# Moving the gate tiles and the gathers, powers and scatters within a loop over 32 experts

## The chip, the cores and the metric

The kernel runs on one core of a Trainium2 chip. The metric is the device time of one execution in microseconds. The kernel before takes 1062.58 us, the median of three runs (1060.21 to 1063.12).

## The reference, cut to what matters

One layer of a streaming encoder for 1024 tokens of width 1024. A mixer (three kinds of heads) adds to `h`; then a mixture of 32 experts adds to it, two experts per token; at the end a gate, computed from the sum, adds an embedding. Only the last two parts matter here.

```python
def hierarchical_moe(h, ...):
    ...
    y = routed_experts(xt, e_idx, e_w, w_gate, w_up, w_down)

def block_ffn(args):
    tok, wt, e = args
    xb = xt[tok]
    hb = jax.nn.silu(xb @ w_gate[e]) * (xb @ w_up[e])
    return (hb @ w_down[e]).astype(F32) * wt[:, None]

def reference(...):
    ...
    h = h + hierarchical_moe(rms_norm(h, norm2_g[i]), ...)
    gate = jax.nn.sigmoid(rms_norm(h, ple_norm_g[i]) @ ple_gate_w[i])
    h = h + gate * (p[i] @ ple_proj_w[i]).astype(F32)
    return rms_norm(h, final_g).astype(x.dtype)
```

A row of the output needs the sum of both its experts, so the gate can be computed for those tokens first whose second expert comes early.

## The kernel before, in words

Up to about 600 us the kernel computes the mixer and the routing. Then comes the stage that the change touches: a loop `for e in range(NE - 1)` over experts 0 to 30 (L1807), and behind it, from 992 us to the end, expert 31 and the last three gate tiles.

**An expert.** Each has at most 128 tokens. `gather` (L1226, GpSimd) fetches their rows from the DRAM tensor `hn2s` into one of three buffers `xg`, three experts ahead. `turned` (L1239) transposes them on TensorE; `up` (24 matmuls, L144 to L146) multiplies by the gate and up weights, `act` applies the activation, `hidden` transposes the result (`ph`, L1258), `down` (12 matmuls) multiplies by the down weight one loop later. `scaled` (L1275, ScalarE) writes the output times the routing weight into `yo`, of which there are two (`NYO`). `scatter` (L1278, GpSimd) adds these rows in DRAM to `h2s`, the sum for all tokens. Each scatter waits for the one before, since both add to the same tensor.

**Weights.** All matmuls take fp16 pairs. A weight arrives in fp32 by a transfer of 1 MB that SyncE issues, into one of the free buffers `ws` or `arena`; `split` then makes the pair: ScalarE the high half (L140), VectorE the low half (L141). A buffer is free again behind the split. `refill(e)`, at the top of the loop, issues as many transfers of the list `parts` as there are free buffers. That list holds the three weights of each expert, in order. `KEEP(e)` says how many buffers `refill` has taken out of this circulation by loop e: they later hold the gate's weight, the projection's weight and the gate tiles (`slot`, `new_set` at the loops in `SETS`).

**The gate.** The gate's weight (four quarters) and the projection of the embedding are split in the loops of `GW` (one loop later, by `GLAG`), a quarter a loop: five extra splits. Tokens are put into the order of their second expert: `ranks` (L1634, L1636, GpSimd) and `ranked` (L1641, TensorE) in loop 2, `reorder` in loops 3 to 6. The tokens form eight tiles of 128. Tile t has a pair (L, C) in `TILES`, and `add` puts its steps at named points of the loops:

- `load` at loop L: two GpSimd gathers by the tile's order (L1692), of the rows of `p` into `pin` and of the rows of `h2s` into `h3`. The second needs the scatters up to expert `AFTER[t]`, and no later one.
- `rms` at L + 2: ScalarE squares (L1709), VectorE scales (L129), GpSimd takes the power (`rg`, L131). `norm` at L + 2: VectorE multiplies (L1713). `embed` at L + 2: two transposes (`ptr`, L1718) and a small split.
- `turned` at C: eight transposes (`h3t`, L1725) and two splits. `mm` at C and C + 1: 24 matmuls each, half a tile. `emb`, `gate`, `square` and `gained` (L1762, GpSimd) beside them.
- `out` at C + 2: another power (`rf`). `send`: L1779 on VectorE and an indirect write to the output (L1783, GpSimd).

Tiles 0 to 4 have their steps in the loop, tiles 5 to 7 behind it.

**The order.** Inside `tc.manual_schedule` every engine runs its instructions in the order in which the program is written. A loop's points are, in order: `refill`, scatter, gather, `up`, point "up", `act`, the next expert's `turned`, point "turned", the last expert's `down`, the first weight split of expert e+2, point "mid", its second split, point "late", `hidden`, point "emb", the split of the down weight, a gate split, `scaled`, point "gate". The scatter in loop e is that of expert e-2, the gather that of expert e+3. GpSimd issues gathers, scatters, tile loads and output writes from one instruction stream, in which the powers and the ranks' adds also stand.

Of the kernel before, what the change touches and what calls it, by code (L numbers as in the profile page):

```python
# [52 lines left out]
MMP = ("mid", "mm")  # L53
AFTERW = 1
HS = 16.0
RMS = (2, "mid")
NORM = (2, "late")
EMB = (2, "mid")
TURN = (0, "up")
PPD = "emb"  # L60
# [1 line left out]
CUT = 320  # L62
NDW = 2
NYO = 2
GW = {6: (0,), 7: (1,), 8: (2,), 9: (3,), 10: (4,)}
GLAG = 1
TAIL = 4
RANK = 2
SETS = (9, 30)
TILES = ((10, 13), (14, 17), (17, 21), (21, 24), (25, 28))  # L70
AFTER = (8, 12, 14, 19, 23, 28, 30)
# [1 line left out]
_p = defaultdict(list)  # L73
def add(k, *ops): _p[k] += ops
for t, (L, C) in enumerate(TILES):
    add((L, "turned"), ("load", t))
    add((L + RMS[0], RMS[1]), ("rms", t))
    add((L + NORM[0], NORM[1]), ("norm", t))
    add((L + EMB[0], EMB[1]), ("embed", t))
    add((C + TURN[0], TURN[1]), ("turned", t))  # L80
    for i in range(2):
        add((C + i, MMP[i]), ("mm", t, i))
        add((C + i, PPD), ("emb", t, i))
        add((C + i, "gate"), ("gate", t, i), ("square", t, i), ("gained", t, 512 * i, 512 * i + 512))
    add((C + 2, OUT), ("out", t))
    add((C + 2, "gate"), ("send", t))
add((30, "turned"), ("load", 5))
PLAN = dict(_p)

KEEP = lambda e: min(8, max(0, e - 4))  # L90
HALVES = {3: (0,), 4: (1,), 5: (2,), 6: (3,), 7: (4, 5), 8: (6, 7)}
FOUR = {mybir.EngineType.PE, mybir.EngineType.Activation, mybir.EngineType.DVE, mybir.EngineType.Pool}

# [2 lines left out]
def hybrid_kernel(ctx, tc, x, p, norm1_g, w_in, conv_w, conv_b, igate_b, fgate_b, mnorm_g, sb_out_g,  # L96
# [27 lines left out]
    def rows(src, n):  # L124
        return bass.AP(tensor=src.tensor, offset=src.offset, ap=[[0, P], [1, n]])
# [1064 lines left out]
    class Expert:  # L1190
# [86 lines left out]
        def scatter(self):  # L1277
            return nc.gpsimd.indirect_dma_start(  # L1278
                out=h2s, out_offset=bass.IndirectOffsetOnAxis(ap=self.tb[:, 1:2], axis=0),
                in_=self.yo, in_offset=None, bounds_check=S - 1, oob_is_err=False, compute_op=OP.add)  # L1280
# [53 lines left out]
    for e in range(NE):  # L1334
        if e + 2 < NE:
            parts += [(e + 2, 0), (e + 2, 1)]
        if e:
            parts += [(e, 2)]
        parts += [(NE, a) for a in GW.get(e, ())]

# [234 lines left out]
    def at_e(e, f, *a):  # L1575
        if 0 <= e < NE:
            getattr(E[e], f)(*a)
# [3 lines left out]
    with tc.If(over > CAP):  # L1581
        with tc.tile_pool(name="ovc", bufs=1, side="right") as ovc:
            xo = ovc.tile([P, 2, KT, P], F16, name="xTo")
            late = ovc.tile([1, 1], F32, name="late")
# [31 lines left out]
    def refill(e):  # L1616
        while retired[0] < KEEP(e) and ready:
            retired[0] += 1
            kept.append(ready.pop(0))
        feed(min(len(ready), len(parts)))  # L1620
# [3 lines left out]
    def slot():  # L1624
        return (kept or ready).pop(0)


    def ranks():
        R.s = yaf[:, :2 * D]
        f = R.s.bitcast(F16).rearrange("p (a t e) -> p a t e", a=8, e=NE)  # L1630
        R.own, R.acc = f[:, 0, :NT], f[:, 1, :NT]
        nc.vector.tensor_copy(R.own[:, :, 0:1], LE[:, :, 0:1])
        nc.vector.tensor_tensor(R.own[:, :, 1:], LE[:, :, 1:], LE[:, :, :-1], op=OP.subtract)
        nc.gpsimd.memset(R.acc[:, 0], 0.0)  # L1634
        for t in range(1, NT):
            nc.gpsimd.tensor_tensor(R.acc[:, t], R.acc[:, t - 1], R.own[:, t - 1], op=OP.add)  # L1636
# [162 lines left out]
    def plan(e, point):  # L1799
        for f, t, *a in PLAN.pop((e, point), ()):  # L1800
            getattr(G[t], f)(*a)

    with tc.manual_schedule(engines=FOUR):
        nc.scalar.activation(jk[:, :1], vf32[:, n, 1, 2:3], AF.Silu)
        E[0].turned()
        E[0].split_d()
        for e in range(NE - 1):  # L1807
            refill(e)
            scatter(e - 2)
            at_e(e + NX, "gather")  # L1810
            if e == RANK:
                ranks()
            if RANK < e <= RANK + 4:
                reorder(2 * (e - RANK - 1), 2 * (e - RANK - 1) + 1)
            if e == RANK + 6:
                nc.gpsimd.dma_start(order, perm.rearrange("(t q) c -> q t c", q=P))
                nc.gpsimd.dma_start(fg, rows(final_g, D))
            E[e].up()
            plan(e, "up")
            E[e].act()  # L1820
            E[e + 1].turned()
            if e == NE - 2:
                E[e + 1].dw = [w.rearrange("p (k n) -> p k n", k=2) for w in slot().bitcast(F16).rearrange("p (a n) -> a p n", a=2)]
                E[e + 1].split_d()
            if e - 1 in SHIFT:
                E[e - 1].split_d()
            plan(e, "turned")
            plan(e, "mm")
            at_e(e - 1, "down")
            if e == RANK:  # L1830
                ranked()
            if e + 2 < NE:
                E[e + 2].split_g(0)
            plan(e, "mid")
            if e + 2 < NE:
                E[e + 2].split_g(1)
            plan(e, "late")
            E[e].hidden()
            plan(e, "emb")
            if e and e not in SHIFT:  # L1840
                E[e].split_d()
            for a in GW.get(e - GLAG, ()):
                gate_w(a) if a < 4 else proj_w()
            if e in SETS:
                new_set()
            at_e(e - 1, "scaled")
            plan(e, "gate")
            plan(e, "end")
        a, z = NE - 2, NE - 1
        scatter(a - 1)  # L1850
        E[z].up()
        E[z].act()
        G[5].embed("7")
        E[a].down()
        E[a].scaled()
        scatter(a)
        E[z].hidden()
        G[5].rms()
        G[5].norm()
        G[6].load(1)  # L1860
        E[z].down()
        E[z].scaled()
        scatter(z)
        G[5].turned("01")
        G[7].load(0, 0)
        G[5].mm(0, "23")
        G[5].emb(0, "7")
        G[5].gate(0)
        G[5].square(0)
        G[6].embed("0")  # L1870
        G[6].rms()
        G[6].norm()
        G[5].mm(1, "23")
        G[5].emb(1, "4")
        G[6].turned("01")
        G[5].gate(1)
        G[5].square(1)
        G[6].mm(0, "23")
        G[6].emb(0, "7")
        G[5].out()  # L1880
        G[5].send()
        G[6].gate(0)
        G[6].square(0)
        G[7].embed("0")
        G[7].rms()
        G[7].norm()
        G[6].mm(1, "23")
        G[6].emb(1, "4")
        G[7].turned("01")
        G[6].gate(1)  # L1890
        G[6].square(1)
        G[7].emb(0, "7")
        G[7].mm(0, "23")
        G[6].out()
        G[6].send()
        G[7].gate(0)
        G[7].square(0)
        G[7].emb(1, "4")
        G[7].summed()
        G[7].gained(0, 512)  # L1900
        G[7].mm(1, "23", (0, CUT, 512))
        G[7].gate(1, 0, CUT)
        G[7].square(1, 0, CUT)
        G[7].more()
        G[7].gained(512, 512 + CUT)
        G[7].gate(1, CUT, 512)
        G[7].square(1, CUT, 512)
        G[7].gained(512 + CUT, D)
        G[7].more()
        G[7].last()  # L1910
# [29 lines left out]
```

## Time and profile before

| | |
|---|---|
| Three runs | 1062.58, 1063.12, 1060.21 us; median 1062.58 us |
| Profiled execution | 1055.94 us, its span 1054.4 us |
| Mean granted TensorE clock | 0.951 |
| Expert loop, hidden transposes of expert 0 to those of expert 30 | 605 to 992 us |
| Behind it, to the end of the span | 992 to 1054 us |

The profile is of one execution; its span is what the hardware profiler recorded of it, from the first instruction to the last, and 1.54 us of its time lie around that. Times below are microseconds from the span's start. Engines are PE (TensorE's matmuls), PEld (its weight loads), DVE (VectorE), ACT (ScalarE), POOL (GpSimd) and SP (SyncE). L1226 is line 1226 of the kernel. The granted clock is given as a share of full speed, 1.00 being 2.4 GHz. In the table of stretches a row has the stretch and its length, then the busy time and the number of instructions of PE, PEld, DVE, ACT and POOL, then TensorE's granted clock, the busy share of the DMA engines and the GB/s that they moved.

### The profile page before, as it was taken

Reading aid. Unit: us, or ns where it says so; the run is one execution under the profiler, and the core shown is the slowest. Engines: PE = TensorE matmul, PEld = TensorE weight load, DVE = VectorE, ACT = ScalarE, POOL = GpSimd, SP = SyncE. Lnnn points to the kernel's source line nnn. Section 1 sums busy time; section 2 is a strip of 40 time slices with the busy share of each in tenths; the row PEclk is TensorE's granted clock in tenths of the full one; section 3 lists DMA queues with packets and bytes.
Section 4 is the critical chain, followed back from the end, with each engine's and each line's share of the span. In section 5 each row is a group of like instructions: output and inputs, shape, how many; then the busy total and the mean of one; then the engine's idle time right before and its main releaser. Section 6 shows DMA issues by size and latency. Waiting matters only on the chain. (4 is left out here: it accounts for less than half of the span.)

```text
span 1054.4 us, 15998 instructions
## 1 busy us (share of the span) xinstructions
PE 929.9 (88%) x5935; PEld 539.9 (51%) x5936; DVE 742.5 (70%) x1267; ACT 582.2 (55%) x937; POOL 429.6 (41%) x383
## 2 busy tenths in 40 slices
PE   7799989989999868989787589997899899999796
PEld 4457855545665445656544445443454454444343
DVE  4443548998988975568878578997576777686333
ACT  4343565454557552344353378997576777585432
POOL 1101224435772443132333638753365435552621
PEclk8999999999999998989997699999899999999898
DMA  6411122123210286855257699999789798896330
GB/s 219 127 31 44 41 56 56 51 71 92 78 57 29 90 236 204 292 161 185 102 180 261 209 326 347 273 330 331 236 268 333 243 323 281 275 336 224 83 85 40
DMA packets 72657, 189.94 MB, mean 180 GB/s; under 512 B 13407, under 2 KB 40637, under 8 KB 64384
## 3 DMA queue, kind: packets, MB, share of 16 engines
q1 hardware_dynamic: 57824, 154.40, 42.8%
q0 software_dynamic: 14608, 33.97, 11.9%
q8 instruction: 47, 0.77, 0.3%
q10 hardware_dynamic: 144, 0.52, 0.1%
q14 instruction: 34, 0.28, 0.1%
HBM read 166.01 MB, written 37.31 MB: 193 GB/s over the span
## 5 line engine op out<-in xcount | busy, mean ns | idle before, releaser
L671 POOL TENSOR_TENSOR a<-a,rest 128x128 f32<-128x128 f32 (+7 forms) x48 | 60.1, 1252 | 162.0 <-DVE rest L670 131.0
L1278 POOL DMA_INDIRECT h2s<-yo,tabs x32 | 71.6, 2239 | 73.0 <-DMA h2s<-yo,tabs 38.9
L144 PE MATMUL pg<-arena,xT 128*128 128x512 f16 x256 | 97.5, 381 | 0.7 <-ACT xT L1240 0.7
L145 PE MATMUL pg<-arena,xT 128*128 128x512 f16 x256 | 97.5, 381 | 0.0
L146 PE MATMUL pg<-arena,xT 128*128 128x512 f16 x256 | 97.5, 381 | 0.0
L141 DVE SCALAR_TENSOR_TENSOR arena<-arena 128x2048 f16<-128x2048 f32 (+1 forms) x39 | 81.3, 2099 | 20.8 <-ACT arena L140 20.8
L670 DVE TENSOR_TENSOR_SCAN rest<-rest,one 128x128 f32<-128x128 f32 (+7 forms) x48 | 75.7, 1576 | 7.0 <-ACT rest L663 6.7
L146 PEld LDWEIGHTS <-arena 128*128 128x128 f16 x516 | 51.5, 100 | 51.2 <-DVE arena L252 6.8
L141 DVE SCALAR_TENSOR_TENSOR arena<-ws,arena 128x2048 f16<-128x2048 f32 x29 | 65.9, 2286 | 14.6 <-ACT arena L140 14.6
L145 PEld LDWEIGHTS <-arena 128*128 128x128 f16 x516 | 51.6, 100 | 39.8 <-issue 11.5
L144 PEld LDWEIGHTS <-arena 128*128 128x128 f16 x516 | 52.1, 101 | 36.1 <-issue 3.8
L140 ACT ACTIVATE arena<-arena 128x2048 f16<-128x2048 f32 (+1 forms) x39 | 67.0, 1738 | 0.0
L140 ACT ACTIVATE arena<-ws 128x2048 f16<-128x2048 f32 x29 | 55.1, 1920 | 0.0
L145 PE MATMUL pd<-dl,hT 128*128 128x512 f16 x120 | 46.9, 391 | 5.2 <-DVE dl L141 5.2
L144 PE MATMUL po<-woh,yT 128*128 128x512 f16 x128 | 50.8, 397 | 0.0
L687 ACT ACTIVATE ah<-at 128x512 f16<-128x512 f32 (+3 forms) x72 | 32.7, 490 | 32.7 <-PE at L680 32.2
L145 PE MATMUL po<-wol,yT 128*128 128x512 f16 x128 | 50.6, 395 | 0.0
L146 PE MATMUL po<-woh,yT 128*128 128x512 f16 x128 | 50.3, 393 | 0.0
L693 DVE TENSOR_TENSOR al<-at,ah 128x512 f16<-128x512 f32 (+3 forms) x72 | 36.8, 538 | 15.5 <-ACT ah L687 15.5
L146 PE MATMUL pd<-dh,hT 128*128 128x512 f16 x120 | 47.0, 392 | 0.0
L144 PE MATMUL pd<-dh,hT 128*128 128x512 f16 x120 | 46.8, 390 | 0.2 <-ACT yo L1275 0.2
L141 DVE SCALAR_TENSOR_TENSOR dl<-arena,dh 128x2048 f16<-128x2048 f32 x17 | 38.9, 2286 | 11.0 <-ACT dh L140 11.0
(662 smaller groups left out, 2730.3 us busy)
## 6 DMA issues: line engine op xcount, KB each, us to landing
arena<-in_w_down_dram SPq DMA_DIRECT2D x19, 1024.0 KB, 10.0
arena<-in_w_up_dram SPq DMA_DIRECT2D x18, 1024.0 KB, 5.1
arena<-in_w_gate_dram SPq DMA_DIRECT2D x17, 1024.0 KB, 8.0
ws<-in_w_gate_dram SPq DMA_DIRECT2D x14, 1024.0 KB, 8.9
ws<-in_w_up_dram SPq DMA_DIRECT2D x13, 1024.0 KB, 11.5
ws<-in_w_down_dram SPq DMA_DIRECT2D x12, 1024.0 KB, 8.5
arena<-in_w_in_dram SPq DMA_DIRECT2D x16, 384.0 KB, 3.4
x<-in_x_dram SPq DMA_DIRECT2D x8, 512.0 KB, 6.4
```

The lines of the kernel that those rows point to most:

```text
L140: nc.scalar.activation(hi, src, AF.Copy, scale=scale)
L141: nc.vector.scalar_tensor_tensor(lo, src, scale, hi, op0=OP.mult, op1=OP.subtract)
L144: nc.tensor.matmul(o, a[0], w[0], start=first, stop=False)
L145: nc.tensor.matmul(o, a[0], w[1], start=False, stop=False)
L146: nc.tensor.matmul(o, a[1], w[0], start=False, stop=last)
L670: nc.vector.tensor_tensor_scan(back, back, one1.to_broadcast([P, n]), 1.0, op0=OP.mult, op1=OP.mult)
L671: nc.gpsimd.tensor_tensor(self.a[:, :n], self.a[:, :n], self.rest[:, w - n + 1:w + 1], op=OP.mult)
L687: nc.scalar.activation(ah[:, :m * P], pt[:, :m * P], AF.Copy)
L693: nc.vector.tensor_tensor(al[:, :m * P], pt[:, :m * P], self.hl[s][:, :m * P], op=OP.subtract)
L1278: return nc.gpsimd.indirect_dma_start(out=h2s, out_offset=bass.IndirectOffsetOnAxis(ap=self.tb[:, 1:2], axis=0), in_=self.yo, in_offset=No ...
```

## The change

All of it moves steps; no instruction is added or removed.

- The splits of the gate's and the projection's weights go three loops on (`GW`), and the buffers for them are taken out of circulation two loops later (`KEEP`); the first set of tile buffers is made in loop 11 instead of 9.
- Tile 0 goes from loops (10, 13) to (12, 15), tile 1 from (14, 17) to (15, 18), tile 2 from (17, 21) to (18, 21). Tiles 3 and 4 keep their loops. All loads go from the point "turned" to "late".
- `rms` goes from "mid" to "turned", `norm` from "late" to "mid".
- The scatter of expert e-2 goes from the top of the loop, ahead of the gather, to behind the point "mid".

```diff
-RMS = (2, "mid")
-NORM = (2, "late")
+RMS = (2, "turned")
+NORM = (2, "mid")
...
-GW = {6: (0,), 7: (1,), 8: (2,), 9: (3,), 10: (4,)}
+GW = {9: (0,), 10: (1,), 11: (2,), 12: (3,), 13: (4,)}
...
-SETS = (9, 30)
-TILES = ((10, 13), (14, 17), (17, 21), (21, 24), (25, 28))
+SETS = (11, 30)
+TILES = ((12, 15), (15, 18), (18, 21), (21, 24), (25, 28))
...
-    add((L, "turned"), ("load", t))
+    add((L, "late"), ("load", t))
...
-add((30, "turned"), ("load", 5))
+add((30, "late"), ("load", 5))
...
-KEEP = lambda e: min(8, max(0, e - 4))
+KEEP = lambda e: min(8, max(0, e - 6))
...
             refill(e)
-            scatter(e - 2)
             at_e(e + NX, "gather")
...
             plan(e, "mid")
+            scatter(e - 2)
             if e + 2 < NE:
                 E[e + 2].split_g(1)
```

On GpSimd, around the loads of tile 0, before (loops 10 to 12). `yo_...` is the output of one expert, here 8, 9 and 10 in turn; `xg_6504`, `xg_6505` and `ya` are the three buffers of gathered expert rows; `ws_6491` is the tile's rows `h3`.

```order
L1278 DMA h2s<-yo_7752,tabs 1024x1024
L1226 DMA xg_6505<-hn2s,tabs 128x2048
L1692 DMA ya<-in_p_dram,order 128x256
L1692 DMA ws_6491<-h2s,order 128x1024
L1278 DMA h2s<-yo_7849,tabs 1024x1024
L1226 DMA ya<-hn2s,tabs 128x2048
L1278 DMA h2s<-yo_7939,tabs 1024x1024
L1226 DMA xg_6504<-hn2s,tabs 128x2048
L131 TENSOR_TENSOR rg0r<-rg0a,nhalf 128x1
```

The same place in the change, loops 11 to 14; the outputs are those of experts 9 to 12.

```order
L1278 DMA h2s<-yo_7831,tabs 1024x1024
L1226 DMA xg_6504<-hn2s,tabs 128x2048
L1278 DMA h2s<-yo_7923,tabs 1024x1024
L1692 DMA ya<-in_p_dram,order 128x256
L1692 DMA ws_6508<-h2s,order 128x1024
L1226 DMA xg_6505<-hn2s,tabs 128x2048
L1278 DMA h2s<-yo_8021,tabs 1024x1024
L1226 DMA ya<-hn2s,tabs 128x2048
L131 TENSOR_TENSOR rg0r<-rg0a,nhalf 128x1
L1278 DMA h2s<-yo_8113,tabs 1024x1024
```

The tile's row gather stood right behind the scatter of expert 8 and now stands behind that of expert 10; the power `rg0r` stood behind a scatter and a gather and now stands behind a gather and ahead of the scatter.

GpSimd again, around the powers of tile 1, before (from loop 15; the outputs are those of experts 13 and 14):

```order
L1278 DMA h2s<-yo_8305,tabs 1024x1024
L1226 DMA xg_6504<-hn2s,tabs 128x2048
L131 TENSOR_TENSOR rf0r<-rf0a,nhalf 128x1
L1783 DMA out_dram<-ws_6491,order 1024x1024
L1278 DMA h2s<-yo_8403,tabs 1024x1024
L1226 DMA xg_6505<-hn2s,tabs 128x2048
L131 TENSOR_TENSOR rg1r<-rg1a,nhalf 128x1
L1278 DMA h2s<-yo_8505,tabs 1024x1024
L1226 DMA ya<-hn2s,tabs 128x2048
```

In the change (from the scatter of loop 16, expert 14; the next output is expert 15's):

```order
L1278 DMA h2s<-yo_8356,tabs 1024x1024
L1762 TENSOR_TENSOR ws_6508<-ws_6508,ya 128x512
L1226 DMA ya<-hn2s,tabs 128x2048
L131 TENSOR_TENSOR rf0r<-rf0a,nhalf 128x1
L131 TENSOR_TENSOR rg1r<-rg1a,nhalf 128x1
L1278 DMA h2s<-yo_8482,tabs 1024x1024
L1783 DMA out_dram<-ws_6508,order 1024x1024
L1226 DMA xg_6504<-hn2s,tabs 128x2048
```

Both powers now stand ahead of their loop's scatter, with one gather between them and the loop's start.

VectorE at tile 1's norm (L1713), before. The rows on `arena` with 128x8x256 are an expert weight's low half, `ya<-ptr` is the embedding's split, `hT` the low half of the hidden rows.

```order
L1240 COPY xT_8444<-xt_8455 128x1024
L141 SCALAR_TENSOR_TENSOR arena<-arena 128x8x256
L129 TENSOR_SCALAR rg1a<-ms_8481 128x1
L141 SCALAR_TENSOR_TENSOR ya<-ptr_8487,ya 128x256
L141 SCALAR_TENSOR_TENSOR arena<-arena 128x8x256
L1713 TENSOR_SCALAR ws_6485<-ws_6491,rg1r 128x1024
L141 SCALAR_TENSOR_TENSOR hT_8498<-ph_8495,hT_8498 128x256
```

In the change:

```order
L1240 COPY xT_8528<-xt_8539 128x1024
L129 TENSOR_SCALAR rg1a<-ms_8549 128x1
L141 SCALAR_TENSOR_TENSOR arena<-ws_6510,arena 128x8x256
L1713 TENSOR_SCALAR ws_6491<-ws_6508,rg1r 128x1024
L141 SCALAR_TENSOR_TENSOR ya<-ptr_8572,ya 128x256
L141 SCALAR_TENSOR_TENSOR arena<-arena 128x8x256
L141 SCALAR_TENSOR_TENSOR hT_8585<-ph_8582,hT_8585 128x256
```

The first scaling (`rg1a`) and the norm now each stand ahead of the weight split that they stood behind.

On GpSimd in loop 2, the ranks' adds (L1636) and the scatter of expert 0, as a difference:

```order
-L1278 DMA h2s<-yo_7005,tabs 1024x1024
 L1226 DMA ya<-hn2s,tabs 128x2048
 L1634 MEMSET ya 128x32
 L1636 TENSOR_TENSOR ya<-ya 128x32 x7
+L1278 DMA h2s<-yo_7005,tabs 1024x1024
```

The scatter stood two instructions ahead of the ranks and now follows them.

## Rows read from the trace of the kernel before

**Rows 1.** TensorE and the other engines over the whole span (the page, part 1).

```profile
PE 929.9 (88%) x5935; PEld 539.9 (51%) x5936; DVE 742.5 (70%) x1267; ACT 582.2 (55%) x937; POOL 429.6 (41%) x383
```

**Rows 2.** The table of stretches (columns named above): loops 4, 10, 12, 13, 14 and 20.

```profile
638.70:647.70 9.00, 9.00 (x56) 4.68 (x55) 7.50 (x7) 7.77 (x9) 6.95 (x5) 1.00 1.02 367
695.20:705.40 10.20, 9.38 (x54) 4.44 (x54) 10.20 (x9) 10.20 (x11) 4.34 (x2) 1.00 0.96 311
716.10:730.70 14.60, 11.01 (x58) 5.28 (x57) 12.17 (x9) 10.06 (x10) 5.32 (x3) 0.88 0.97 366
730.70:754.10 23.40, 17.28 (x89) 9.55 (x87) 13.18 (x13) 12.53 (x14) 6.56 (x5) 0.85 0.76 251
754.10:769.40 15.30, 15.30 (x85) 7.60 (x84) 9.62 (x8) 9.44 (x11) 7.45 (x4) 1.00 0.62 197
832.30:844.20 11.90, 9.14 (x56) 4.63 (x55) 10.49 (x11) 10.26 (x12) 6.96 (x4) 1.00 0.78 246
```

**Rows 3.** What TensorE waited for, 605 to 992 us (total us, times, longest us).

```profile
PE h3t L1725 <- issue: 6.1, 1, 6.1
...
PE xt L1239 <- DMA xg<-hn2s,tabs: 5.2, 2, 3.6
PE h3t L1725 <- DVE ws L1713: 4.8, 3, 1.6
...
PE rank L1641 <- POOL ya L1636: 2.6, 1, 2.6
```

**Rows 4.** GpSimd in order of time, loops 11 to 13 (start, us, instruction, idle before).

```profile
710.02 1.70 POOL L1278 DMA_INDIRECT h2s<-yo,tabs  x1 [6.53 <-DMA h2s<-yo,tabs]
712.03 1.70 POOL L1226 DMA_INDIRECT xg<-hn2s,tabs  x1 [0.31 <-issue]
...
722.29 1.77 POOL L1692 DMA_INDIRECT ws<-h2s,order  x1 [6.20 <-DMA ws<-in_w_up_dram]
724.36 2.51 POOL L1278 DMA_INDIRECT h2s<-yo,tabs  x1 [0.31 <-issue]
...
737.24 2.27 POOL L1278 DMA_INDIRECT h2s<-yo,tabs  x1 [9.02 <-DMA h2s<-yo,tabs]
...
740.86 0.60 POOL L131 TENSOR_TENSOR rg0r<-rg0a,nhalf 128x1 f32<-128x1 f32 x1
```

**Rows 5.** ScalarE in order of time: tile 0's square.

```profile
732.50 1.06 ACT L1709 ACTIVATE jk<-ws 128x1024 f16<-128x1024 f32 x1 [3.72 <-DMA ws<-h2s,order]
```

**Rows 6.** GpSimd in order of time, before tile 1's norm.

```profile
789.03 3.30 POOL L1278 DMA_INDIRECT h2s<-yo,tabs  x1 [0.31 <-issue]
...
795.02 0.58 POOL L131 TENSOR_TENSOR rg1r<-rg1a,nhalf 128x1 f32<-128x1 f32 x1
```

**Rows 7.** VectorE in order of time, the same stretch.

```profile
790.78 0.15 DVE L129 TENSOR_SCALAR rg1a<-ms 128x1 f32<-128x1 f32 x1
790.84 0.42 DVE L141 SCALAR_TENSOR_TENSOR ya<-ptr,ya 128x256 f16<-128x256 f32 x1
...
795.63 0.75 DVE L1713 TENSOR_SCALAR ws<-ws,rg1r 128x1024 f32<-128x1024 f32 x1 [1.56 <-POOL rg1r L131]
```

**Rows 8.** GpSimd and VectorE in order of time, around the ranks.

```profile
620.58 3.27 POOL L1278 DMA_INDIRECT h2s<-yo,tabs  x1 [6.93 <-ACT yo L1275]
...
625.42 2.17 POOL L1636 TENSOR_TENSOR ya<-ya 128x32 f16<-128x32 f16 x7
...
622.32 0.28 DVE L1633 TENSOR_TENSOR ya<-gv 128x248 f16<-128x248 f16 x1
```

**Rows 9.** The DMA table for loops 1 to 11, 605 to 727 us.

```profile
DMA packets 9747, 39.20 MB, mean 321 GB/s; under 512 B 2405, under 2 KB 2421, under 8 KB 7525
...
q0 software_dynamic: 3680, 7.67, 24.2%
```

**Rows 10.** GpSimd in order of time, two scatters near tile 3.

```profile
897.28 3.63 POOL L1278 DMA_INDIRECT h2s<-yo,tabs  x1 [0.30 <-issue]
...
911.84 1.59 POOL L1278 DMA_INDIRECT h2s<-yo,tabs  x1 [1.43 <-DMA h2s<-yo,tabs]
```

## The prediction

> **What bounds the kernel now.** The page comes first: TensorE is busy for 88% of the span [rows 1], so what an edit can return is its idle time, stage by stage. The change lies in the loop over 32 experts, from 605 us to 992 us. I therefore read the table of stretches next, with borders at the starts of the `hidden` transposes (L1258), so that the stretch of loop e runs from expert e-1's transposes to expert e's [rows 2]. A loop with nothing but an expert takes 9.0 us and has TensorE busy for all of it (loop 4). While the quarters of the gate's weight are split a loop takes 10.2 us, and DVE and ACT are busy for all of it (loop 10): there those two are the bound. A loop with half a gate tile takes 15.3 us, TensorE busy throughout (loop 14). Against these three prices loops 12, 13 and 20 stand out: 14.6, 23.4 and 11.9 us.
>
> The table of waits says what TensorE waited for [rows 3]: 5.2 us for gathered rows of experts, 6.1 us at the first transposes of tile 0, 4.8 us (three times) at those of tiles 1, 3 and 4, 2.6 us for the ranks. GpSimd's order of time says why [rows 4]. Each scatter waits until the one before has landed: the one issued at 710.02 had landed when the gather from the same tensor began at 722.29, 12.3 us later (the row names a weight's transfer; I take it for the scatter, which the program makes the gather wait for); from 724.36 to 737.24 it is 12.9 us. A gather of an expert's rows stands behind a scatter, so it inherits that wait. Tile 0's row gather, 722.29, kept ACT waiting 3.72 us at the square [rows 5], and its power came at 740.86, behind scatter 10 and a gather.
>
> **The change, part by part.** Matmuls, splits, transfers and bytes are the same in number; all of it moves work.
>
> *Tile 0 moves from loop 13 to 15, and its loads to behind the scatter of loop 12.* Its row gather needs scatter 8 alone, which before had just been issued and now is two scatters old. Loaded in loop 12 and squared in loop 14, it has a loop and a half instead of one and a half minus a scatter's 12.3 us. The 6.1 us wait, and the slow clock behind it (0.85 granted over loop 13, so part of it at 1.2 instead of 2.4 GHz [rows 2]), should go: 23.4 - 15.3 = **8.1 us**.
>
> *Gathers ahead of scatters.* GpSimd's sequence is rotated: the gather for expert e+3 now follows scatter e-3, not e-2. In the stretch where a scatter takes over 12 us that is some 10 us sooner, more than the longest wait, 3.6 us [rows 3]. Loop 12 goes from 14.6 to the 10.2 of a loop with gate splits: **4.4 us**. The waiting gather (712.03 [rows 4]) ran while the DMA engines were busy for 0.97 of loop 12 [rows 2]. [...]
>
> *Powers ahead of scatters, square and norm half a loop sooner.* For tile 1 the power's input was ready at 790.9, and the power ran at 795.02, behind scatter 14 (3.3 us) and a gather [rows 6, 7]. Now only the gather is ahead, and DVE's norm stands before the second weight split instead of behind it. The norm, at 795.63 before [rows 7], moves ahead by 2.3 us for the split and by more for the scatter, which covers the 1.6 us waits: 4.8 us. Loop 20 (tile 2, the same power behind the same scatter) can go from 11.9 to 9.0: 2.9 us. Some wait for the low half of the down weights is left in each loop, 0.2 us or so; I take **7.0 us**. If DVE's total is the limit there, as little as 1 us.
>
> *Ranks ahead of scatter 0.* Their seven adds took 2.17 us from 625.42, behind a scatter that waited for its output until 620.58; the input was there at 622.6 [rows 8]. They end at about 625, when TensorE comes: up to 2.6 us. But scatter 0 starts some 4 us later and all the scatters behind it follow. I take **1.5 us**, bounds 0 and 2.6.
>
> *The tile's small work now meets the last gate splits.* Square (1.06 us on ACT [rows 5]), norm (0.75) and the split of the embedding's input (0.4) fall into loop 14, behind the fourth quarter and beside the projection's split. ACT and DVE have no room there (loop 10). Cost **2.0 us**, bounds 1 and 3; before, they lay in loop 13, where both were idle.
>
> *Three experts more before the first tile.* A tile loop is where the DMA queue catches up: its share is 0.62 in loop 14, and 0.95 or more in loops 10 and 12 [rows 2]. Now loops 12 to 14 bring no such relief. Each of three experts needs three weights of 1.049 MB and about 0.73 MB of gather and scatter (7.67 MB for ten or eleven of them [rows 9]): 11.6 MB. TensorE wants them in 27 us (3 x 9.0). At the mean rate of loops 1 to 11, 321 GB/s [rows 9], they take 36.1 us, 9.1 too long; at the best loop's 367 GB/s (loop 4), 31.6, which is 4.6 too long. It may cost nothing: two more buffers stay with the stream until loop 14, and what held it before was as much a free buffer as the rate. By the scatters, three at 12.3 to 12.9 us take 37 to 39 us, 10 to 12 too long, and since a scatter must have landed before the output buffer is written again two experts later, ACT would stop for that. These lie side by side, not in a row. I take **6.0 us**, bounds 0 and 12.
>
> *At nothing:* moving the last load (tile 5) to `late`, since on GpSimd it still stands behind scatter 28 and a power. The work after the loop is unchanged. The loads of tiles 3 to 5 still follow the scatter that they need, as before; GpSimd stands there, but no one waits for it.
>
> Sum: 8.1 + 4.4 + 7.0 + 1.5 - 2.0 - 6.0 = **13.0 us less**. The profiled execution took 1055.94 us, 6.6 below the median of the runs, 1062.58; the gain comes off either, so 1042.9 for such an execution and 1049.6 for the median, which I forecast.
>
> **The rivals.**
> - *Nothing new binds in loops 12 to 14.* For it: the stream was short of buffers as well as of rate, and gets two for longer; loop 4 moved 367 GB/s. Against it: the shares of 0.95 and more. The last cost is 0: 19.0 us less, 1043.6.
> - *The waits only move.* Tile norms come in time, but TensorE then waits for the low half of the down weights, one step on; or the gathers gain nothing; or the backlog is at its upper bound. Each takes 4 to 6 us off: about 7 us less, 1055.6.
> - *It fills up.* Two of these together leave 0 to 3 us: 1061.
> - *Slower: the chain of scatters sets the pace.* Place: loops 7 to 14, on GpSimd, then ACT's write of the output buffer. Two buffers give the chain about one loop, 10 us. Eight scatters at t us each, against 3 x 9.0 + 5 x 10.2 = 78 us of loops, stall 8t - 88. For it: scatter 0 starts later, and one pair stands 14.5 us apart, landing awaited (897.28 to 911.84 [rows 10]). Against it: 12.3 to 12.9 in the worst stretch before [rows 4]. At 14.5 the stall is 28 instead of 6: 9 us slower, 1071.6. It decides from 13.4 us on, where the stall eats the other 19.0.
> - *The change does not do what it says:* the instruction order shows the gathers, powers and scatters exchanged, so I give this nothing.
>
> **How the numbers follow.** The forecast has 0.50, no backlog 0.20, the waits that move 0.18, filled up 0.06, the scatter chain 0.06. A measurement of this kernel tells 0.3%, 3.2 us, from no change; that is below 1059.4 for faster. The first three are faster: 0.88. The fourth is within: 0.06; the last is slower: 0.06. I shift a little, 0.86, 0.09, 0.05, since the third can end close to the line and the last just short of it. The range takes in no backlog with ranks in full (21 us less) and the waits that move with half of the rest lost (4 us less): 1041.5 to 1058.5.
>
> **What would show it.** Right: no wait for gathered rows on TensorE before expert 16; no wait at the first transposes of a tile above 0.5 us, tiles 0 to 4; the rank wait under 0.5 us; loops 12 to 15 together longer than their work by some 6 us, with ACT waiting for a weight's landing or a scatter. Wrong: TensorE waits of 3 us or more in loops 10 to 15 with the clock falling behind them (the backlog is larger); the norm waits still there (GpSimd was not what held them); scatters 13 us and more apart in a row, with ACT waiting before the scaled output (the slower case); or a new wait in the tiles' loops, of which I see none now.

## The result, and the profile after

The change takes 1048.78 us, the median of eight runs (1042.61 to 1053.43). The kernel before, in eight runs, takes 1058.35 us: five more runs brought its median 4.2 us below the 1062.58 of the first three. The ratio is 0.9922 (95% interval 0.9895 to 0.9948): 8.3 us faster by that ratio, with an interval of 5.5 to 11.1; the two medians differ by 9.6. The profiled execution took 1049.17 us, its span 1047.6.

Part 1 of the page, which answers to [rows 1]: TensorE is busy for 5 us less, at the same number of instructions.

```profile
PE 924.7 (88%) x5935; PEld 538.7 (51%) x5936; DVE 743.4 (71%) x1267; ACT 581.6 (56%) x937; POOL 422.4 (40%) x383
```

What the two traces give by stage is worked out from the starts of the `hidden` transposes (L1258). "Behind loop 30" begins at expert 30's transposes, in the kernel before at 980.0 us; the 992 us given above are those of expert 31. Tile 0's matmuls are done by the end of loop 16 in both; its output stands in loop 15 before and in loop 17 after.

| Stretch | before, us | after, us | difference | forecast |
|---|---|---|---|---|
| up to expert 0's hidden transposes | 605.1 | 606.0 | +0.9 | 0 |
| loops 1 to 6 | 61.0 | 58.2 | -2.8 | -1.5 |
| loops 7 to 16 | 123.3 | 121.1 | -2.2 | -4.5 |
| loops 17 to 30 | 190.7 | 188.7 | -2.0 | -7.0 |
| behind loop 30 | 74.4 | 73.6 | -0.8 | 0 |
| span | 1054.4 | 1047.6 | -6.8 | -13.0 |

The table of stretches of the change, for loops 7 to 14, loop 15 (the first half of tile 0), loop 16 (the second) and loop 18 (the first half of tile 1); it answers to [rows 2].

```profile
core 0: us, PE busy (x) PEld busy (x) DVE busy (x) ACT busy (x) POOL busy (x), PEclk, DMA share, GB/s
664.20:749.10 84.90, 74.26 (x436) 37.60 (x434) 72.98 (x56) 71.30 (x72) 39.32 (x24) 1.00 0.90 296
749.10:769.90 20.80, 17.04 (x86) 8.18 (x87) 17.36 (x15) 15.80 (x16) 6.49 (x4) 0.92 1.00 351
769.90:785.30 15.40, 15.40 (x86) 7.61 (x85) 9.62 (x8) 9.44 (x11) 9.27 (x6) 1.00 0.87 314
795.70:812.20 16.50, 15.24 (x88) 7.89 (x87) 15.22 (x13) 12.02 (x13) 7.85 (x4) 1.00 0.83 255
```

Loop 16 costs 15.4 us, about what loop 14 did before (15.3). Loop 15 takes 20.8 where 15.3 would do: TensorE waits in it for 1.4, 1.4 and 0.9 us, and at a granted clock of 0.92 its work takes 17.0. Loops 7 to 14 take 84.9.

What TensorE waited for between 605 and 990 us answers to [rows 3]; columns as there.

```profile
engine line waited for: us in total, times, longest us
PE pd L144 <- ACT yo L1275: 9.0, 9, 1.6
PE pd L145 <- DVE dl L141: 7.6, 12, 0.9
PE xt L1239 <- DVE hT L141: 5.6, 11, 1.4
PE h3t L1725 <- DVE ya L141: 1.4, 1, 1.4
```

The waits for gathered rows, for the ranks and for the norm (L1713) are gone, and tile 0's wait has fallen from 6.1 to 1.4 us. In their place stand 9.0 us for `yo` (0.2 before). The waits for the low half of the down weights and for that of the hidden rows have grown, to 7.6 and 5.6 us; before they were:

```profile
PE pd L145 <- DVE dl L141: 5.2, 12, 0.9
...
PE xt L1239 <- DVE hT L141: 2.9, 2, 1.8
```

ScalarE's waits in loops 1 to 15 say what is behind the 9.0 us:

```profile
ACT yo L1275 <- DMA h2s<-yo,tabs: 12.5, 7, 3.4
...
ACT jk L1709 <- DMA ws<-h2s,order: 2.0, 1, 2.0
```

ScalarE waited seven times for a landed scatter before it could write the output. GpSimd and ScalarE in order of time, loops 7 to 9:

```profile
672.90 1.58 POOL L1278 DMA_INDIRECT h2s<-yo,tabs  x1 [0.30 <-ACT yo L1275]
...
683.03 1.58 POOL L1278 DMA_INDIRECT h2s<-yo,tabs  x1 [7.18 <-ACT yo L1275]
...
693.10 2.06 POOL L1278 DMA_INDIRECT h2s<-yo,tabs  x1 [5.54 <-ACT yo L1275]
...
704.13 1.60 POOL L1278 DMA_INDIRECT h2s<-yo,tabs  x1 [7.61 <-ACT yo L1275]
```

```profile
682.32 1.26 ACT L1275 ACTIVATE yo<-pd,tabs 128x512 f32<-128x512 f32 x2 [2.74 <-DMA h2s<-yo,tabs]
...
692.32 1.26 ACT L1275 ACTIVATE yo<-pd,tabs 128x512 f32<-128x512 f32 x2 [1.89 <-DMA h2s<-yo,tabs]
...
703.39 1.26 ACT L1275 ACTIVATE yo<-pd,tabs 128x512 f32<-128x512 f32 x2 [2.95 <-DMA h2s<-yo,tabs]
```

The output at 682.32 goes into the buffer that the scatter at 672.90 read, and could be written 9.4 us after that scatter's issue; from 683.03 to 692.32 it is 9.3, from 693.10 to 703.39 it is 10.3. The next scatter follows within a microsecond of each landing. (GpSimd's rows name ScalarE's output as releaser; the output in question had been written 10 us before, so it was the landing.) So here a scatter goes off every 10 to 11 us (10.7 on the mean from scatter 4 to 12), and with two output buffers the loops cannot go on being shorter than that.

### The profile page after: what moved, and what is told of

Its sections match the earlier page's. It is cut to its first block, busy times and chain, and to the rows that moved or that the text cites. A ratio compares the mean times of both kernels' runs of the same rounds, so it can differ in the third digit from the quotient of the medians.

```text
span 1047.6 us, 15991 instructions
## 1 busy us (share of the span) xinstructions
PE 924.7 (88%) x5935; PEld 538.7 (51%) x5936; DVE 743.4 (71%) x1267; ACT 581.6 (56%) x937; POOL 422.4 (40%) x383
## 3 DMA queue, kind: packets, MB, share of 16 engines
q0 software_dynamic: 14608, 33.97, 11.7%
## 5 line engine op out<-in xcount | busy, mean ns | idle before, releaser
L1278 POOL DMA_INDIRECT h2s<-yo,tabs x32 | 67.6, 2113 | 86.6 <-ACT yo L1275 39.5
L141 DVE SCALAR_TENSOR_TENSOR arena<-ws,arena 128x2048 f16<-128x2048 f32 x35 | 79.5, 2289 | 19.4 <-ACT arena L140 19.4
L141 DVE SCALAR_TENSOR_TENSOR arena<-arena 128x2048 f16<-128x2048 f32 (+1 forms) x34 | 68.8, 2036 | 15.9 <-ACT arena L140 15.9
L141 DVE SCALAR_TENSOR_TENSOR dl<-ws,dh 128x2048 f16<-128x2048 f32 x26 | 59.5, 2287 | 13.7 <-ACT dh L140 13.7
L140 ACT ACTIVATE arena<-ws 128x2048 f16<-128x2048 f32 x35 | 66.3, 1918 | 0.0
L140 ACT ACTIVATE arena<-arena 128x2048 f16<-128x2048 f32 (+1 forms) x34 | 57.6, 1708 | 0.0
L144 PE MATMUL pd<-dh,hT 128*128 128x512 f16 x120 | 45.9, 383 | 8.2 <-ACT yo L1275 8.2
L1275 ACT ACTIVATE yo<-pd,tabs 128x512 f32<-128x512 f32 x64 | 40.5, 687 | 18.1 <-DMA h2s<-yo,tabs 16.6
L140 ACT ACTIVATE dh<-ws 128x2048 f16<-128x2048 f32 x26 | 49.8, 1914 | 0.0
```

The costliest lines, as they stand in the source:

```text
L140: nc.scalar.activation(hi, src, AF.Copy, scale=scale)
L141: nc.vector.scalar_tensor_tensor(lo, src, scale, hi, op0=OP.mult, op1=OP.subtract)
L144: nc.tensor.matmul(o, a[0], w[0], start=first, stop=False)
L1275: nc.scalar.activation(self.yo[:, nh * 512:nh * 512 + 512], pd, AF.Copy, scale=self.tb.bitcast(F32)[:, 2:3])
L1278: return nc.gpsimd.indirect_dma_start(out=h2s, out_offset=bass.IndirectOffsetOnAxis(ap=self.tb[:, 1:2], axis=0), in_=self.yo, in_offset=No ...
```

## The experiments

The theory at the start was that **the chain of scatters** paces loops 7 to 14: one landing per loop. The first rival was the forecast's own cause for this term, full engines and a late weight stream. Each ratio below is against the kernel before. Medians of before were 1056.6 to 1057.8 us in these batches.

To compare runs, the table gives for each profile how far behind expert 0's hidden transposes the scatters of experts 1, 4, 8 and 12 (S1 to S12) were issued, and the length of three stretches, in us.

| Kernel | S1 | S4 | S8 | S12 | loops 1-6 | loops 7-14 | loop 15 |
|---|---|---|---|---|---|---|---|
| before (tile 0 in loop 13) | 28.0 | 61.2 | 104.9 | 157.5 | 61.0 | - | - |
| the change | 31.2 | 66.9 | 106.9 | 152.7 | 58.2 | 84.9 | 20.8 |
| e1, four outputs | 31.2 | 66.9 | 106.0 | 152.3 | 58.2 | 82.1 | 24.0 |
| e5, points back | 31.2 | 66.9 | 107.3 | 152.7 | 58.2 | 85.3 | 17.6 |
| e6, load ahead | 31.2 | 66.9 | 106.2 | 152.0 | 58.2 | 84.8 | 17.8 |
| e7, scatter 0 first | 31.4 | 69.8 | 109.8 | 154.0 | 60.2 | 85.3 | 19.3 |
| e9, reorder behind | 28.9 | 63.8 | 107.0 | 152.2 | 58.2 | 84.6 | 19.7 |
| e10, three moves | 30.7 | 66.5 | 108.1 | 152.2 | 58.2 | 85.7 | 17.0 |
| e11, and four outputs | 30.5 | 66.7 | 105.9 | 151.0 | 58.2 | 84.0 | 18.7 |
| e12, and scatter 0 first | 29.1 | 63.9 | 105.4 | 150.1 | 59.6 | 85.6 | 19.1 |

**Four output buffers (e1).** From expert 6 on, half of the outputs lie in a weight buffer.

```diff
-            self.yo = self.wx.tile([P, D], F32, ...)
+            if self.e != "o" and self.e >= 5 and self.e % 4 > 1:
+                self.yo = more_yo[0][:, self.e % 2 * D:self.e % 2 * D + D]
+            else:
+                self.yo = self.wx.tile([P, D], F32, ...)
...
-KEEP = lambda e: min(8, max(0, e - 6))
+KEEP = lambda e: min(8, max(0, e - 6) + (e > 4))
...
             refill(e)
+            if e == 5:
+                more_yo.append(slot())
```

> The change with four output buffers yo instead of two: from expert 6 on, half of the experts write theirs into the halves of one weight buffer, which leaves the stream in loop 5. Chain theory (scatters follow each other 10 to 12.8 us apart, so ScalarE may not write the output and TensorE waits for it): ScalarE's 12.5 us of waits for a landed scatter and TensorE's 9.0 us for yo both go, loops 7 to 14 fall from 84.9 us to about 80; but the scatters keep their pace, so tile 0's row gather, behind scatter 10, falls behind the loops and the first transposes of tile 0 wait some 4 us more: in all -3 to +1 us against the change. Split theory (the excess of loops 7 to 14 is ScalarE and VectorE filled with gate splits, or weights that come late): loops 7 to 14 stay within 1 us of 84.9, other waits take the place.

1050.09 us, ratio 0.9915 (0.9884 to 0.9945): no different from the change. The waits moved as the chain theory says. ScalarE's, up to 770 us, and TensorE's, up to 990 us:

```profile
ACT jk L1712 <- DMA ws<-h2s,order: 7.1, 1, 7.1
ACT yo L1278 <- DMA h2s<-yo,tabs: 3.4, 2, 3.0
```

```profile
PE h3t L1728 <- DVE ya L141: 5.8, 1, 5.8
...
PE pd L144 <- ACT yo L1278: 3.1, 2, 2.0
```

ScalarE's wait for a landing fell from 12.5 to 3.4 us, TensorE's for `yo` from 9.0 to 3.1, loops 7 to 14 from 84.9 to 82.1, while the square of tile 0 (now L1712) waited 7.1 us for the tile's rows instead of 2.0, and loop 15 grew to 24.0. Loops 7 to 13 fell from 74.1 to 68.9 us: loops 9 to 11 ran at 8.9 to 9.5 us, as loops 4 to 6 do, loops 12 and 13, behind a gate split, at 10.3, and loops 7 and 8 at 10.2 and 10.4, with waits of 1.2 us each. The DMA engines were busier there than in the change, 0.93 against 0.88, and ScalarE waited for no weight. So neither full engines nor weights held those. But the scatters kept their times to 1.7 us up to number 12, and tile 0's row gather stands behind them: what the outputs gave back, the tile's rows took.

**The parts alone (e2, e3, e4).** Three experiments put one part of the change each on the kernel before. First (e2) the scatter behind the gather, with the loads at "late":

```diff
-            scatter(e - 2)
             at_e(e + NX, "gather")
...
             plan(e, "mid")
+            scatter(e - 2)
```

> The kernel before with one part of the change: the scatter behind the gather and the powers (behind the point mid), and the tile loads at late, since they need that scatter. Part-by-part theory: the rank wait of 2.6 us, the waits for gathered rows of 5.2 us and, with the powers early, up to half of the norm waits (4.8 us) go; scatter 0 is 5 us later, so tile 0's row gather is later by as much and its wait of 6.1 us grows to 8 to 11: in all -3 to -7 us against before. Rival (order on GpSimd matters little, since the chain of scatters paces everything): within 2 us of before.

1051.64 us, ratio 0.9931 (0.9906 to 0.9956): 7.3 us faster, nearly all that the whole change gives. What TensorE waited for:

```profile
PE h3t L1725 <- issue: 7.7, 1, 7.7
PE pd L144 <- ACT yo L1275: 6.7, 5, 2.1
...
PE h3t L1725 <- DVE ws L1713: 1.5, 3, 0.5
```

No wait for ranks or gathered rows is left, and the norm waits fell from 4.8 to 1.5 us, although square and norm kept their old points. Tile 0's wait grew to 7.7, and `yo` costs 6.7: the chain binds here as well.

Then square and norm alone (e3):

```diff
-RMS = (2, "mid")
-NORM = (2, "late")
+RMS = (2, "turned")
+NORM = (2, "mid")
```

> The kernel before with one part of the change: square at turned, norm at mid. The power still stands behind a scatter and a gather. Part-by-part theory: no gain by itself, since the power keeps its time; VectorE waits for it ahead of the second weight split instead of behind it, so the split comes 1 to 3 us later at each of five tiles: 0 to +6 us. Rival (the place of the norm on VectorE was what held tiles 1, 3 and 4): -3 to -5 us.

1061.99 us, ratio 1.0035 (1.0011 to 1.0060): 3.7 us slower, as the theory had it. Loops 17 to 30 took 197.0 us instead of 190.7.

Then `GW`, `SETS`, `TILES`, `KEEP` and the loads alone (e4), with the edits as in the change.

> The kernel before with one part of the change: tiles 0 to 2, the gate's splits and the buffers for them moved as in the change, loads at late; scatter ahead of the gather, and square and norm as before. Part-by-part theory: the 6.1 us wait of tile 0 and the slow clock behind it go (-6 to -8 us), the waits for gathered rows stay or grow in loops 11 to 14, because GpSimd's gather stands behind a scatter that is late (+0 to +4), and the norm waits stay: -3 to -8 us. Rival (the chain of scatters takes it back in loops 7 to 14): within 2 us of before.

1058.07 us, ratio 1.0011 (0.9990 to 1.0032): nothing, the rival's case.

```profile
PE xt L1239 <- DMA xg<-hn2s,tabs: 10.0, 5, 3.5
...
PE h3t L1725 <- issue: 4.3, 1, 4.3
```

The waits for gathered rows doubled from 5.2 to 10.0 us, with the gathers still behind the scatters, and tile 0's wait only fell to 4.3. In this trace nearly all scatters from 1 to 13 were issued within 0.8 us of the landing of the one before. Moving the tiles alone gives nothing that these runs show. What it is worth with the gathers ahead of the scatters, e2 and the next experiment tell: 3.1 us by their ratios, whose intervals overlap, and 2.6 from expert 0's transposes to the end of the profiles.

**Square and norm back, in the change (e5).**

> The change with square and norm put back to mid and late. VectorE theory (with the power early, the norm ahead of the second split only pushes that split and the down weight's low half back, so TensorE waits 0.93 and 0.33 us for them at each of tiles 1 to 4 where it would wait 0.5 us for the norm): 1.5 to 3 us faster than the change. Rival (the early points are needed once the power is early; the norm waits of 1.6 us come back at tiles 1 to 4): 1 to 4 us slower than the change.

1045.90 us, ratio 0.9902 (0.9871 to 0.9933), against 0.9922 for the change; the intervals overlap, so the total alone doesn't settle it; the loops say more. VectorE at tile 1's norm in the change, and with the points back:

```profile
798.79 0.75 DVE L1713 TENSOR_SCALAR ws<-ws,rg1r 128x1024 f32<-128x1024 f32 x1
...
799.79 2.28 DVE L141 SCALAR_TENSOR_TENSOR arena<-arena 128x2048 f16<-128x2048 f32 x1
801.99 0.42 DVE L141 SCALAR_TENSOR_TENSOR hT<-ph,hT 128x256 f16<-128x256 f32 x1
802.32 2.28 DVE L141 SCALAR_TENSOR_TENSOR dl<-ws,dh 128x2048 f16<-128x2048 f32 x1
```

```profile
790.12 2.29 DVE L141 SCALAR_TENSOR_TENSOR arena<-arena 128x2048 f16<-128x2048 f32 x1 [0.42 <-ACT arena L140]
792.33 0.75 DVE L1713 TENSOR_SCALAR ws<-ws,rg1r 128x1024 f32<-128x1024 f32 x1
...
793.33 2.28 DVE L141 SCALAR_TENSOR_TENSOR dl<-ws,dh 128x2048 f16<-128x2048 f32 x1
```

In the change the norm and the embedding's split push the second weight split (799.79) and with it the low halves at 801.99 and 802.32; TensorE waits 0.33 and 0.93 us for those. With the points back the split goes first, the norm is ready at 793.1, and TensorE waits 0.51 us for it and 0.26 for the low half of the down weight. The first loop of tiles 1 to 4 takes 16.1 instead of 16.5 us, and loop 15 takes 17.6 instead of 20.8. Loops 17 to 30 together gain only 0.6 us, as loop 27 and tile 4 have other waits here. The points were moved for a wait of which the scatter's place removes most by itself.

**Loads of tiles 0 to 2 ahead of the scatter (e6).**

```diff
-    add((L, "late"), ("load", t))
+    add((L, "turned" if t < 3 else "late"), ("load", t))
```

> The change with the loads of tiles 0 to 2 at turned, ahead of the loop's scatter, so that tile 0's row gather stands behind scatter 9 instead of 10, in time when GpSimd only waits for landings. Chain theory: the gather leaves some 8 us sooner; ScalarE's wait of 2.0 us at the square goes, the stretch of loop 15 falls from 20.8 us to 18 or 19; the scatters' pace and the 9.0 us of waits for yo stay: -2 to -3 us against the change. Rival (loop 15 is full because VectorE has the projection's split, the tile's splits and the experts' there): loop 15 stays within 1 us of 20.8, no gain.

Loop 15 fell to 17.8 us, as expected, and ScalarE no longer waits for tile 0's rows. The total, 1048.40 us, ratio 0.9921 (0.9891 to 0.9951), shows nothing of it; an interval of 6 us can't tell 3 us.

**Scatter 0 ahead of the ranks' adds (e7).**

```diff
             if e == RANK:
+                scatter(0)
                 ranks()
...
-            scatter(e - 2)
+            if e != RANK:
+                scatter(e - 2)
```

> The change with scatter 0 alone put back ahead of the ranks' adds, where GpSimd stood idle for 6.7 us. Chain theory: scatter 0 starts 5 us sooner and so do all scatters to number 13; TensorE's waits for yo in loops 7 to 14 fall from 9.0 to 3 to 6 us and tile 0's rows come sooner; the rank wait comes back with 1 to 2.6 us: -4 to 0 us against the change. Rival (the later scatters are held by something else than the chain's start, so it catches up): only the rank wait comes back, +1 to +3 us.

1052.33 us, ratio 0.9951 (0.9921 to 0.9981): 3 us worse than the change, though the intervals overlap; from expert 0's transposes to the end the profile is 0.8 us longer. No gain in either, so the rival's case. GpSimd in order of time:

```profile
624.15 3.27 POOL L1278 DMA_INDIRECT h2s<-yo,tabs  x1 [5.63 <-ACT yo L1275]
...
627.64 2.18 POOL L1636 TENSOR_TENSOR ya<-ya 128x32 f16<-128x32 f16 x7
630.35 1.06 POOL L1226 DMA_INDIRECT xg<-hn2s,tabs  x1 [0.53 <-PE rank L1641]
...
640.09 3.53 POOL L1278 DMA_INDIRECT h2s<-yo,tabs  x1 [0.30 <-ACT arena L140]
```

Scatter 0 went off 15.5 us behind expert 0's transposes instead of 20.4, but scatter 1 came at 31.4, where the change has 31.2: the gather at 630.35 and the reorder's casts and writes filled the 10 us ahead of it. The theory in this form, that the chain's start decides, falls. The eighth run (e8) was the kernel of e1 once more:

> The change with four output buffers, again, for one look: as the first experiment, loops 7 to 14 at about 82 us and the stretch of loop 15 at about 24 us.

It gave 82.0 and 23.8 us for these two stretches, and 1052.07 us in its one run.

**The reorder behind the scatter (e9).** The theory was now that GpSimd's order in loops 3 to 6 sets the lag.

```diff
-            if RANK < e <= RANK + 4:
-                reorder(...)
...
             scatter(e - 2)
+            if RANK < e <= RANK + 4:
+                reorder(...)
```

> The change with one step moved: in loops 3 to 6 the reorder (two casts and two indirect writes on GpSimd) behind the scatter instead of ahead of it. Order theory (scatters 1 to 4 are late because GpSimd works through gather and reorder ahead of each, 10 to 12 us a loop, and the chain of landings keeps that lag to tile 0): scatter 4 stands 62 us behind the hidden transposes of expert 0 instead of 67; TensorE's waits for yo in loops 7 to 14 fall from 9.0 us to 3 to 5, and tile 0's row gather is 3 to 5 us sooner: -3 to -6 us against the change. Rival (the landings alone set the pace, 10 to 11 us apart in any order): scatter 4 within 2 us of 67, waits and time as in the change.

1047.24 us, ratio 0.9915 (0.9887 to 0.9943). Scatter 4 came 3 us sooner, at 63.8, and TensorE's waits for `yo` fell from 9.0 to 6.7 us, but scatter 8 was at 107.0 and scatter 12 at 152.2, where the change has them: the lead was lost in four steps. This trace has the landings themselves: scatters 4 to 13 were each issued 0.75 to 0.79 us behind the landing of the one before, which came 8.5 to 11.7 us after its own issue. So the landings set the pace, as the rival has it, although scatter 4 did move by more than 2 us.

**Three moves, then four outputs, then scatter 0 first (e10, e11, e12).** Reorder behind, points back, loads ahead, in one kernel; then the same with the edit of e1; then with that of e7 as well.

> The change with three moves: the reorder behind the scatter, square and norm back at mid and late, the loads of tiles 0 to 2 at turned. If they add: -2.5 us from the points, 0 to -3 from the load, -3 to -6 from the reorder, so -6 to -11 us against the change and 0.98 to 0.985 of before. If the chain of landings takes it back: as the points alone, 0.99 of before.

1044.94 us, ratio 0.9906 (0.9877 to 0.9934): as the points alone, the second case.

> The same three moves with four output buffers. Chain theory: no wait of ScalarE for a landed scatter in loops 6 to 14 and, with the load ahead of the scatter, no wait for tile 0's rows over 1 us: loops 7 to 14 at 79 to 81 us, loop 15 at 16 to 18 us: 2 to 5 us faster than the three moves alone. Rival (one weight buffer less from loop 5 on, and scatters that fall behind until tiles 1 and 2 wait for their rows): within 1.5 us of the three moves alone, or slower.

1040.26 us in six runs, ratio 0.9856 (0.9810 to 0.9902). The fastest median here, but the table of stretches, for loops 7 to 14 and loop 15, doesn't bear the theory out:

```profile
658.60:742.60 84.00, 74.94 (x435) 37.72 (x434) 73.42 (x56) 72.99 (x73) 52.36 (x28) 0.98 0.96 317
742.60:761.30 18.70, 15.46 (x88) 7.89 (x87) 16.00 (x14) 14.65 (x16) 6.84 (x5) 1.00 0.95 327
```

84.0 and 18.7 us sum to 102.7, as the three moves alone do (85.7 and 17.0). The wait for `yo` is only later, in loops 14 and 15, and there ScalarE now also waits for weights to land, for 7.7 us in four waits, as the rival with one weight buffer less expects. From expert 0's transposes to the end the profiles have 438.3 us here, 437.4 with three moves, 441.6 in the change, 449.3 before. Whether the outputs add something is open.

> The three moves with four output buffers, and scatter 0 ahead of the ranks' adds as in the seventh run; now no reorder stands between scatter 0 and scatter 1. Chain theory (the chain runs from scatter 0 at one landing a step, and GpSimd's order held scatter 1 in the seventh run): scatter 1 stands 27 to 28 us behind the hidden transposes of expert 0 instead of 30.3, scatter 8 some 3 us sooner than its 105.9; TensorE's waits for yo (6.9 us from loop 7 on) fall to 2 to 5 us, against 1.3 us of rank wait that come back: -3 to +1 us against the run with the three moves and four buffers. Rival (landings grow longer when scatters come earlier, among full DMA engines, so the chain catches up by scatter 8): scatter 8 within 1 us of 105.9, +1 to +2 us.

1044.09 us, ratio 0.9881 (0.9837 to 0.9926). Scatter 8 came at 105.4, within 0.5 us of the run before: the rival's case. The loss is larger than either named: 3.8 us in the medians and 3.1 from expert 0's transposes to the end, of which the rank wait is 1.3; ScalarE's waits for weights grew to 8.8 us.

## Why the prediction was right, and where it was not

The time lay in the range and 0.8 us from the forecast, which is partly luck: the gain was 8.3 us by the ratio and 9.6 by the medians, not 13.0, and the median of before came down by 4.2. The lower end of the range is mis-added (no backlog with ranks in full is 20.1 us less, 1042.5, not 21), which decides nothing here. By the steps of the prediction:

- **Tile 0, 8.1 us.** The wait went from 6.1 to 1.4 us, and loop 13 no longer stands out. But part of the slow clock moved along: 0.85 in loop 13 before, 0.92 in loop 15 now. And the step does not stand alone, as the sum has it: without the new order on GpSimd it gave nothing (e4).
- **Gathers, 4.4 us.** As forecast: no wait for gathered rows is left, though the DMA engines were busy for 0.90 of loops 7 to 14. e2 has the same with the tiles in their old places. The Trainium skill says (DMA: Bandwidth & Descriptors, Issuing engines are not separate DMA queues) that DMAs of all issuing engines run on the same 16 engines and interleave. Busy as those were, gathers that were issued sooner came in time here.
- **Powers and norms, 7.0 us. This step failed**: loops 17 to 30 gave 2.0. The powers did come early, but the prediction let the norm move ahead of the weight split for 0.2 us or so a loop. Each tile's wait of 1.6 us became waits of 0.33 and 0.93, here TensorE at tile 1:

```profile
802.46 1.05 PE L1239 MATMUL xt<-identh,xg 128*128 128x128 f16 x16 [0.33 <-DVE hT L141]
...
804.66 0.38 PE L145 MATMUL pd<-dl,hT 128*128 128x512 f16 x1 [0.93 <-DVE dl L141]
```

Loops 20 and 21, from which 2.9 us were to come, take 26.9 us together in both. That is the rival "the waits only move", which named the low half of the down weights. At tiles 1 to 4 TensorE waited 8.4 us in all before, and the step left it 0.7; it is 5.0 in the change and 2.8 with the points back (e5). So the norm's place explains some 2 of the missing 5.0 us, although loops 17 to 30 of e5 return only 0.6 of it, as other waits came up there; e3 has the same sign, those points alone cost 3.7 us. Loop 20 explains another 1.4: it could not fall to 9.0, since tile 1's output now stands in it, and it takes 10.4 without a wait. The rest goes with the 2.8 us that TensorE waits even with the points back.

- **Ranks, 1.5 us.** Mis-sized: the whole wait went, and loops 1 to 6 became 2.8 us shorter, since the delay of scatter 0 cost them nothing yet. The adds end at 625.9:

```profile
623.68 2.17 POOL L1636 TENSOR_TENSOR ya<-ya 128x32 f16<-128x32 f16 x7 [6.66 <-DVE ya L1633]
626.42 1.65 POOL L1278 DMA_INDIRECT h2s<-yo,tabs  x1 [0.57 <-issue]
```

- **The tile's small work in loop 14, cost 2.0 us.** Mis-sized: loop 15 stands 5.5 us above its price, 3.8 in waits and 1.7 by the slow clock. Either taking the points back (e5, 3.2 us) or the rows sooner (e6, 3.0 us) returns over half.
- **Three experts more, cost 6.0 us.** Mis-sized by 1 to 2 us: loops 7 to 14 take 6.9 us more than the 78 at which the prediction prices them, and TensorE's waits for `yo` there, one in each loop, sum to 8.2. (The 78 has one loop with a gate split too many: VectorE's gate splits lie in loops 11 to 15.) The cause was the other one named there: not weights, for which ScalarE never waited in loops 1 to 15, but the scatters. The slower rival had this mechanism with 14.5 us a step; it was 10.7 from scatter 4 to 12 (85.8/8 in the change), short of the 13.4 from which it decides. At 10.7 its formula, 8t - 88, gives no stall at all. It counts on a lead of 10 us from the two buffers, most of which was gone when loop 7 began: scatter 4, which belongs to loop 6, went off 8.7 us behind that loop's end.
- **At nothing:** the part behind loop 30 gave 0.8 us. Expert 31's stretch is 3.4 us shorter (8.7 instead of 12.1), as TensorE's wait for tile 5's rows of `p` fell from 2.2 to 0.2, but tile 5 then waits 6.1 us for its norm instead of 3.5.

Of the signs named in advance most came: no wait for gathered rows or ranks, none at the first transposes of tiles 1 to 4, and loops 12 to 15 together 6.5 us above their work. Two went the other way: tile 0's wait of 1.4 us is above the 0.5 named, and the tiles' loops have the new waits of 0.33 and 0.93.

## What to carry to other kernels

A chain in which each step waits for the landing of the one before sets a floor per loop; give its length a price of its own, from issue to landing, before adding up what can be saved around it, since savings beside it only move the wait (from the gathers to the output buffer, from there to the tile's rows). A late input is best mended at the one instruction that holds it: here the place of the scatter on GpSimd did nearly all, and a second edit against the same wait moved most of it to another engine. Where several parts are changed at once, each alone on the old kernel and each taken back from the new one tell more than the sum.

## What was not expected of the hardware

The landings caught up with every lead tried here, 3 to 5 us. In the ten kernels of the table scatter 8 was issued 104.9 to 109.8 us behind expert 0's transposes, whether scatter 1 had gone at 28.0 or 31.4. Where scatter 4 went 3 us sooner (e9, e12), the next four steps took 43.2 and 41.5 us instead of the change's 40.0. Eight of the traces have the landings. In them scatter 0 landed 26.9 to 29.9 us behind expert 0's transposes, whether it was issued at 15.5 (e3, e4, e12) or at 20.4 (e1, e2, e9, e10, e11): the earlier one took 11.9 to 13.7 us to land, the later one 6.5 to 9.5. Why is open; the DMA engines were busy for 0.95 of loops 1 to 6 in e12. The chain can't simply be cut by dropping its waits: the Trainium skill (DMA: Bandwidth & Descriptors, Rules for kernel authors) says that an accumulating DMA reads its destination and writes it later, so that another write between is lost. No run here tried it.

The stage ahead of the loop, which no kernel changes, moves together with the granted clock. Over the same 42.7 us of the change and of e10 the clock is 0.88 in one and 0.96 in the other, and expert 0's transposes come at 606.0 and at 601.4. In the fourteen profiles they come between 600.3 and 608.7; up to there the mean clock is 0.946 in the three earliest and 0.933 to 0.941 in the others. That is much of why totals here tell 3 us badly. Stretches from a common start tell it better: e1 and e8, the same kernel, have 442.5 and 442.2 us from there to the end.

```profile
517.30:560.00 42.70, 36.64 (x234) 20.99 (x233) 32.83 (x108) 18.63 (x34) 13.21 (x14) 0.88 0.54 185
```

```profile
517.30:560.00 42.70, 35.53 (x258) 19.25 (x257) 35.50 (x128) 18.41 (x34) 15.72 (x18) 0.96 0.61 216
```
